# Two feed-forward units prepared twelve products sooner, and another order of copies, loads and transposes in the first row tiles

## The chip, the cores and the metric

One NeuronCore of a Trainium2 chip runs the kernel. A core has a matrix engine (TensorE, "PE"), three engines for elementwise work (VectorE "DVE", ScalarE "ACT", GpSimd "POOL"), a sync engine ("SP") that here only issues transfers, and 16 DMA engines. Every engine works off its own list of instructions in order; a transfer is issued by an engine and then runs by itself. The metric is the device time of one execution in microseconds, the median of several. Less is better.

## The reference

Two-branch encoder block, one layer, 1024 tokens of 1024 features, all in float32:

```python
h = rmsnorm(x, norm_mix)
q, k, v, r, lr_f, lr_b, u, g_a, g_b = split(h @ w_in)
o = gla(q, k, v, decay(lr_f)) + gla_backward(q, k, v, decay(lr_b))   # 4 heads, chunks of 64
y_a = (rmsnorm_per_head(o) * gla_norm * silu(r)) @ w_branch_gla
y_b = (pool_2_4_8_16(u) @ w_pool_group) * pool_scale                 # 4 channel groups
x = x + (sigmoid(g_a) * y_a + sigmoid(g_b) * y_b) @ w_out
gate, up = split(rmsnorm(x, norm_ffn) @ w_ffn_in)                    # 2816 wide each
x = x + (silu(gate) * up) @ w_ffn_out
return rmsnorm(x, norm_final)
```

## The kernel before

**Arithmetic.** A float32 operand is kept as two reduced-precision parts: `hi`, its cast (made on ACT), and `lo`, the difference between it and `hi` (made on DVE or POOL). One product of two operands is then three matmuls, hi·hi, lo·hi (or hi·lo) and the other cross product; `products` (L291) issues these three, and `mm3` calls it and then `pump`. Larger products use the Strassen–Winograd scheme of seven smaller products, for which sums and differences of the operands' quarters are made first.

**Order of the work.** The program is written out by a Python script whose main thread is the list of matmuls. Everything else hangs on generators that `pump(dt)` moves forward each time a triple of matmuls is issued: `dt` is the width over 512, so a triple of 512 columns is worth 1, and one of 288 columns 0.56. `begin(gen, delay)` puts a generator in the list `side`: it starts after `delay` of such credit, and each number it yields is the credit until its next step. `prepare_beside(jobs, every, put, lag, eng)` puts one in the list `aside`, a step per `every` of credit. `finish_side()` and `finish_beside()` issue at once all that is left of either list. So a number such as `every` sets where in each engine's list an instruction stands; how long it takes or waits there is another matter.

**First row tiles (0 to 47 us).** x arrives in eight tiles of 128 rows, `load_x(t)`. `norm_x(t)` scales a tile by its norm. `to_features` (L352) transposes two neighbouring tiles on PE, in four steps of four transposes (L338), and after each step `gain_and_split` makes the `hh` parts (ACT, L345) and `hl` parts (DVE, L348) of two feature tiles. `first_values` (L414) multiplies one row tile by the 288 columns of `w_in` that hold 256 values of the first head and 32 low-rank decay columns (`VL`, eight triples of 288 columns), and then takes the sum out of its PSUM bank: `vh` (ACT), `vl` (DVE, L199), and `lr`, four copies of the low-rank rows (ACT, L421). The low-rank columns of the weights come as one tile, `lraw` (L384, 128 KB in runs of 128 bytes), apart from the values' columns (`raw`), and POOL splits them (L249) into the `fwh` and `fwl` tiles that ACT and POOL also fill with the values' part. While `first_values` of t=1 runs, `to_features` of tiles 2 and 3 runs beside it, and so on by pairs.

**Gate units (381 to 582 us).** Ten units of seven products each; a product is 12 triples of 512 columns. Units 0 and 1 (kind "u") make the pooling branch's input, 2 to 5 the gate of branch A, 6 to 9 that of branch B. `Gates.run(p)` takes a product's bank: `ga` is filled by a copy on ACT (L1277), by an addition on DVE (L1282), by a sigmoid on ACT (L1285). Units of kind "b" also multiply the pooled rows `ph`, `pl` (loaded back from `p_out` by `load_pooled`, L1219) by the group's weights `wph`, `wpl` into a bank `yb`. The unit's weights come by SP in blocks named `fraw` too (L914 waits for one and makes the sum `fs`); their `wh` parts are casts on ACT (L198).

**Feed-forward units prepared ahead.** `unit_jobs(n)` (L559) is the job list of one feed-forward unit: load two raw tiles `fraw` (512 KB each, on SP), two blank steps, then seven jobs that make the operands of the unit's seven products. `beside` (L607) turns each job into steps: an optional sum or difference on POOL, `lag` steps later a cast `uph` (ACT, L627), a step later the difference `upl` (DVE, L618), and a step later (`put` = 1) the two stores to the DRAM tile `u_out` (L614) on the queue of the engine `eng`, here ACT's. `uph` and `upl` share a ring of five buffers (tag t2) with the rows of the pooling. Two units (`READY` = 2) are prepared this way; the feed-forward stage reads them back some 200 us later. At the start of unit 7 of the gates this list is begun; before the last unit `finish_beside()` empties it.

The lines of the gate loop that set this:

```python
for n, run in enumerate(gate_runs):
    last = n == len(gate_units) - 1
    if n == 7:
        finish_side()
        finish_beside()
        prepare_beside(map(unit_jobs, range(READY)), 3.1, 1, 2, nc.scalar)
    if last:
        finish_beside()
    for at, (of, p) in enumerate(run):
        zs[of].run(p)
```

After the gates come branch A's projection and the merge (582 to 770 us), the feed-forward units (770 to about 1180 us) and the output projection with the final norm (to 1393 us).

Of the kernel before, what the change touches and what calls it, by code (L numbers as in the profile page):

```python
# [52 lines left out]
def kernel(  # L53
# [57 lines left out]
    def as_f32(ap):  # L111
        return ap.bitcast(F32)
# [74 lines left out]
    def begin(gen, delay=0.0):  # L187
        side.append([gen, delay])
# [8 lines left out]
    def split_to(hi, lo, src, eng=nc.vector):  # L197
        nc.scalar.copy(hi, src)  # L198
        eng.tensor_tensor(lo, src, as_f32(hi), op=ALU.subtract)  # L199
# [149 lines left out]
                lo[:, c], src, g, as_f32(hi[:, c]), op0=ALU.mult, op1=ALU.subtract  # L349
            )  # L350

    def to_features(xn, t0, act, gain):  # L352

        for kp in range(KT // 2):
            ps = bank(ps_g, "tr")
            for i in range(2):
                transpose_tile(ps, xn[i], i, kp)
            gain_and_split(ps, kp, t0, act, gain)
            yield 1


    xt = [slot(shape=(D,), s="x") for _ in range(4)]
# [7 lines left out]
    def load_x(t):  # L370
        nc.sync.dma_start(xt[t % 4][:, :], x[t * P : (t + 1) * P, :])

    def load_rows(tile, at, v, n):
        nc.sync.dma_start(tile[at : at + n, :], v[0].rearrange("(j p) -> j p", p=P))
# [4 lines left out]

    load_x(0)  # L380
    load_rows(rows[0], 0, norm_mix, 8)
    load_x(1)
    first_raw = load(*next(order))
    nc.sync.dma_start(lraw[:, :, :], w_in[:, LR0:U0].rearrange("(k p) c -> p k c", p=P))  # L384
    for t in (2, 3):
        load_x(t)
    for i, (v, n) in enumerate(vec_rows):
# [27 lines left out]
    def first_values(w, v, t):  # L415

        ps = bank(ps_mm)
        for kt in range(KT):
            mm3(ps[:, :VL], tokens(hT(kt, t // 4), t), w(kt), kt == 0, kt == KT - 1)
        split_to(*(part[:, t % 4, :] for part in v[t // 4]), ps[:, :DV])  # L420
        nc.scalar.copy(low_rows[:, t, :, :], ps[:, DV:VL].unsqueeze(1).broadcast_to([P, 4, 2 * RANK]))  # L421

    def transpose_low(t):

# [44 lines left out]
    for t in range(0, NT, 2):  # L469
        if t + 4 < NT:  # L470
            begin(norms(t + 4), 1)
        if t == 2:
            for d, w_up in enumerate((w_decay_up_fwd, w_decay_up_bwd)):
                for i in range(3):
                    load_up(i, d, w_up)
            fetch()
        first_values(w, v, t)
        finish_side()
        if t == 0:
            vectors(1, 8)  # L480
        if t + 2 < NT:
            begin(to_features(xn[(t + 2) % 4 :], t + 2, hT, g_mix), 0.5)
        first_values(w, v, t + 1)
        finish_side()
        if t == 4:
            up_weights()
            prepare()
# [38 lines left out]
        return w[k0 : k0 + 2 * P, c_half * HALF : (c_half + 1) * HALF].rearrange("(k p) c -> p k c", p=P)  # L526


    def loading(srcs, tiles):
        def loads():  # L530
            for t, src in zip(tiles, srcs):
                nc.sync.dma_start(t, src)

        yield loads, None, None
        for _ in range(2):
            yield None, None, None


# [21 lines left out]
    def unit_jobs(n):  # L560
        raw = [slot(F32, (KT, P), "fraw")[:, :, :] for _ in range(2)]
        a11, a12, a21, a22 = (t[:, 4 * j : 4 * j + 4, :].rearrange("p k c -> p (k c)") for t in raw for j in range(2))
        yield from loading(
            [w_ffn_in[:, c0 : c0 + P].rearrange("(k p) c -> p k c", p=P) for c0 in (f_order[n] * P, D_FF + f_order[n] * P)], raw
        )
        for op, p, src in (
            (None, 4, a22), (None, 1, a11), (None, 2, a12), (partial(padd, a22, a21, a22), 5, a22),
            (partial(psub, a21, a11, a21), 7, a21), (partial(psub, a11, a22, a11), 6, a11),
            (partial(psub, a12, a12, a11), 3, a12),
        ):  # L570
            yield op, src, u_out[n][p]
# [33 lines left out]
    def beside(jobs, every, put, lag, eng):  # L605

        casts, differ = [None] * lag, None  # L607
        puts = [[] for _ in range(put)]
        while True:
            job = next(jobs, None)  # L610
            if not any((job, *casts, differ, *puts)):
                return
            for pair in puts.pop(0):
                eng.dma_start(*pair)  # L614
            puts.append([])
            if differ:
                src, (hi, lo), dst = differ
                nc.vector.tensor_tensor(lo, src, as_f32(hi), op=ALU.subtract)  # L618
                if len(src.shape) == 2:
                    puts[-1] += [(dst[:, i, :], as_f32(t)) for i, t in enumerate((hi, lo))]  # L620
                else:
                    right.setdefault(dst, []).append((hi, lo))
            differ, cast = None, casts.pop(0)
            if cast:
                src, dst = cast
                parts = parts_for(src)
                nc.scalar.copy(parts[0], src)  # L627
                differ = src, parts, dst
            casts.append(None)
            if job:  # L630
                op, src, dst = job
                if op:
                    op()  # L633
                if src is not None:
                    casts[-1] = src, dst
                elif dst is not None:

                    puts[-1].append((dst, op.args[0]))
            yield every
# [677 lines left out]
    for n, run in enumerate(gate_runs):  # L1317
        zs[n] = Gates(n)
        last = n == len(gate_units) - 1
        if n == 0:  # L1320
            prepare_beside(map(output_jobs, range(4)), 2.8, eng=nc.scalar)
        if n == 7:
            finish_side()
            finish_beside()
            prepare_beside(map(unit_jobs, range(READY)), 3.1, 1, 2, nc.scalar)
        if last:
            finish_beside()
        for at, (of, p) in enumerate(run):
            if not gates_ahead.step() and at in (5, 7):
                line_make()  # L1330
            zs[of].run(p)
            if at in (1, 2) and not last:
                gunits[n + 1].load()
            if p in (7, 4):
                zs[of].store(int(p == 4))
            if at == 4:
                flush(nc.scalar)
                if n == 2:
                    begin(pooling(), 4)
            if 5 <= n < 9 and at == 5:  # L1340
                load_pool_weights(n - 5)
            elif n >= 6 and at == 2:
                split_pool_weights(n - 6)
            if n >= 6 and at == (0 if last else 3):
                load_pooled(n - 6)
            if last and at == 1:
                load_block(0, 0)
                line_load()
                line_load()
                load_block(1, 0)  # L1350
            elif last and at == 2:
                line_load()
                line_load()
                load_block(0, 1)
                load_block(1, 1)
# [534 lines left out]
```

## Time and profile before

| what | value |
|---|---|
| time, median of 3 runs | 1395.01 us (1394.94 to 1395.22) |
| time of the profiled execution | 1394.28 us |
| its span (first to last instruction) | 1392.6 us |
| PE busy | 1366.0 us (98%) in 6654 instructions |
| ACT busy | 624.4 us (45%) |
| DVE busy | 844.0 us (61%) |
| POOL busy | 750.8 us (54%) |
| mean granted TensorE clock | 0.997 of full |

The profiled execution thus spent 1.68 us outside its span, and lies 0.73 us under the median. PE is busy nearly throughout, so whatever the change brings or costs must show as idle time of PE, as matmuls at a lower clock, or as a change in the number of matmuls. The profile gives each of them by place: the waits by engine and what ended them, the windows by stretch of time with their granted clock, the timeline by instruction.

### The profile page before, as it was taken

Reading aid. Unit: us, or ns where it says so; the run is one execution under the profiler, and the core shown is the slowest. Engines: PE = TensorE matmul, PEld = TensorE weight load, DVE = VectorE, ACT = ScalarE, POOL = GpSimd, SP = SyncE. Lnnn points to the kernel's source line nnn. Section 1 sums busy time; section 2 is a strip of 40 time slices with the busy share of each in tenths; the row PEclk is TensorE's granted clock in tenths of the full one; section 3 lists DMA queues with packets and bytes.
Section 4 is the critical chain, followed back from the end, with each engine's and each line's share of the span. In section 5 each row is a group of like instructions: output and inputs, shape, how many; then the busy total and the mean of one; then the engine's idle time right before and its main releaser. Section 6 shows DMA issues by size and latency. Waiting matters only on the chain.

```text
span 1392.6 us, 18505 instructions
## 1 busy us (share of the span) xinstructions
PE 1366.0 (98%) x6654; PEld 1153.0 (83%) x6654; DVE 844.0 (61%) x1073; ACT 624.4 (45%) x1125; POOL 750.8 (54%) x565
## 2 busy tenths in 40 slices
PE   7999999999999999999999999999999999999997
PEld 6889899988888888788887888888888888888876
DVE  6276767767635875587874866555655556343363
ACT  6364655644334444454346533333333334453253
POOL 3260716312397545568664276666766667454354
PEclk9999999999999999999999999999999999999999
DMA  6221422321486668997415455555444447975461
GB/s 192 76 81 37 126 72 96 121 77 46 137 274 233 207 204 275 332 404 261 151 61 212 140 178 174 174 174 168 154 138 143 149 141 265 386 257 210 166 237 66
DMA packets 167452, 243.56 MB, mean 175 GB/s; under 512 B 10904, under 2 KB 97856, under 8 KB 167360
## 3 DMA queue, kind: packets, MB, share of 16 engines
q1 hardware_dynamic: 154944, 216.16, 46.5%
q10 hardware_dynamic: 12416, 26.22, 5.1%
q8 instruction: 52, 0.85, 0.2%
q14 instruction: 40, 0.33, 0.1%
HBM read 164.48 MB, written 77.86 MB: 174 GB/s over the span
## 4 chain that ended last, share of the span: by engine, by line
PE 80%; DVE 5%; issue 5%; POOL 4%; DMA 3%; ACT 2%; SPq 0%; ACTq 0%; POOLq 0%; DVEq 0%
PE ps L291 74%; POOL wl L199 2%; PE op L845 2%; PE kv L291 1%; PE sc L773 1%; DMA wor<-t_out 1%; DMA u_out<-uph 1%; PE op L291 1%; PE tp L1004 1%; DVE fs L914 0%; DMA raw<-in_w_in_dram 0%; DMA ph<-p_out 0%; DVE x L1568 0%; PE yb L291 0%; POOL wsum L633 0%
## 5 line engine op out<-in xcount | busy, mean ns | idle before, releaser
L199 POOL TENSOR_TENSOR wl<-fs,wh 128x512 fp32r<-128x512 f32 x120 | 164.9, 1379 | 164.1 <-ACT wh L198 136.2
L291 PE MATMUL ps<-gh,wh 128*128 128x512 f32 x616 | 240.7, 391 | 0.0
L291 PE MATMUL ps<-gl,wh 128*128 128x512 f32 x616 | 240.1, 390 | 0.4 <-DVE gl L1484 0.4
L291 PE MATMUL ps<-gh,wl 128*128 128x512 f32 x616 | 240.1, 390 | 0.0
L199 POOL TENSOR_TENSOR wl<-fraw,wh 128x512 fp32r<-128x512 f32 x90 | 129.9, 1444 | 66.1 <-ACT wh L198 65.3
L199 POOL TENSOR_TENSOR ol<-gor,oh 128x1024 fp32r<-128x1024 f32 (+1 forms) x42 | 100.3, 2394 | 93.0 <-ACT oh L198 70.4
L291 PE MATMUL ps<-hh,wh 128*128 128x512 f32 x376 | 150.1, 399 | 0.0
L199 POOL TENSOR_TENSOR wl<-raw,wh 128x512 fp32r<-128x512 f32 x44 | 64.0, 1470 | 158.1 <-ACT wh L198 158.1
L291 PE MATMUL ps<-hh,wl 128*128 128x512 f32 x376 | 146.8, 390 | 0.0
L291 PE MATMUL ps<-hl,wh 128*128 128x512 f32 x376 | 146.7, 390 | 0.0
L291 PEld LDWEIGHTS ps<-gl,wh 128*128 128x128 f32 x616 | 115.7, 188 | 24.5 <-DVE gl L1484 0.8
L291 PEld LDWEIGHTS ps<-gh,wl 128*128 128x128 f32 x616 | 115.7, 188 | 24.3 <-DMA wl<-u_out 0.4
L291 PEld LDWEIGHTS ps<-gh,wh 128*128 128x128 f32 x616 | 115.7, 188 | 23.8 <-DMA wh<-u_out 0.3
L291 PE MATMUL ps<-oh,oh 128*128 128x512 f32 x308 | 120.1, 390 | 1.2 <-DVE x L1812 1.2
L291 PE MATMUL ps<-ol,oh 128*128 128x512 f32 x308 | 120.1, 390 | 0.2 <-DVE ol L199 0.2
L291 PE MATMUL ps<-oh,ol 128*128 128x512 f32 x308 | 120.0, 390 | 0.0
L199 POOL TENSOR_TENSOR wl<-wraw,wh 128x512 fp32r<-128x512 f32 x56 | 90.2, 1638 | 47.5 <-ACT wh L198 47.3
L199 DVE TENSOR_TENSOR ol<-wor,oh 128x1024 fp32r<-128x1024 f32 (+1 forms) x42 | 62.2, 1501 | 53.7 <-ACT oh L198 46.4
L198 ACT CAST wh<-fs 128x512 fp32r<-128x512 f32 x120 | 73.8, 615 | 30.8 <-DVE fs L914 23.1
L291 PEld LDWEIGHTS ps<-hh,wl 128*128 128x128 f32 x376 | 70.6, 188 | 14.9
L291 PEld LDWEIGHTS ps<-hh,wh 128*128 128x128 f32 x376 | 70.9, 189 | 13.3
L291 PEld LDWEIGHTS ps<-hl,wh 128*128 128x128 f32 x376 | 70.9, 189 | 13.2
(258 smaller groups left out, 3171.0 us busy)
## 6 DMA issues: line engine op xcount, KB each, us to landing
fraw<-in_w_ffn_in_dram SPq DMA_DIRECT2D x44, 512.0 KB, 6.4
gor<-g_out SPq DMA_DIRECT2D x35, 512.0 KB, 7.4
raw<-in_w_in_dram SPq DMA_DIRECT2D x48, 256.0 KB, 3.5
g_out<-s SPq DMA_DIRECT2D x44, 256.0 KB, 2.3
fraw<-in_w_in_dram SPq DMA_DIRECT2D x20, 512.0 KB, 5.1
wor<-t_out SPq DMA_DIRECT2D x20, 512.0 KB, 7.9
g_out<-g SPq DMA_DIRECT2D x33, 256.0 KB, 2.5
x<-in_x_dram SPq DMA_DIRECT2D x16, 512.0 KB, 4.4
```

The lines of the kernel that those rows point to most:

```text
L198: nc.scalar.copy(hi, src)
L199: eng.tensor_tensor(lo, src, as_f32(hi), op=ALU.subtract)
L291: nc.tensor.matmul(ps, a[i], b[j], start=first and n == 0, stop=last and n == 2, skip_group_check=onto)
L773: nc.tensor.matmul(sc[d][:, i * CH : (i + 1) * CH], chunk_of(ke, n, d), chunk_of(qe, n, d), start=True, stop=True,)
L845: nc.tensor.matmul(op[:, :DV], a, b, start=False, stop=j == len(terms) - 1)
L1004: nc.tensor.transpose(tp[:, i * P : (i + 1) * P], o_heads[j // 2][half][:, i, (j % 2) * P : (j % 2 + 1) * P], ident[:, :],)
```

## The change

Four things are moved; no operation is added or left out.

1. The two feed-forward units are begun twelve triples of matmuls sooner: after the fifth product of gate unit 6 in place of the start of unit 7. A step comes every 2.7 credits, not 3.1; the cast follows the sum by one step, not two; after a unit's load there are four blank steps, not two. The `hi` store is issued right behind its cast, and the `lo` store alone is left to a step later.
2. `lraw` is loaded ahead of x's second tile and of the first weights.
3. In `first_values`, `lr` is copied right after `vh`; `vl` is written out behind it.
4. In `to_features` of tiles 2 and 3 the first step starts after 2.2 credits, not 0.5, and the next ones follow by 0.6, not 1.

```diff
@@ -349,14 +349,14 @@
                 lo[:, c], src, g, as_f32(hi[:, c]), op0=ALU.mult, op1=ALU.subtract
             )
 
-    def to_features(xn, t0, act, gain):
+    def to_features(xn, t0, act, gain, every):
 
         for kp in range(KT // 2):
             ps = bank(ps_g, "tr")
             for i in range(2):
                 transpose_tile(ps, xn[i], i, kp)
             gain_and_split(ps, kp, t0, act, gain)
-            yield 1
+            yield every
 
 
     xt = [slot(shape=(D,), s="x") for _ in range(4)]
@@ -379,9 +379,9 @@
 
     load_x(0)
     load_rows(rows[0], 0, norm_mix, 8)
+    nc.sync.dma_start(lraw[:, :, :], w_in[:, LR0:U0].rearrange("(k p) c -> p k c", p=P))
     load_x(1)
     first_raw = load(*next(order))
-    nc.sync.dma_start(lraw[:, :, :], w_in[:, LR0:U0].rearrange("(k p) c -> p k c", p=P))
     for t in (2, 3):
         load_x(t)
     for i, (v, n) in enumerate(vec_rows):
@@ -417,8 +417,10 @@
         ps = bank(ps_mm)
         for kt in range(KT):
             mm3(ps[:, :VL], tokens(hT(kt, t // 4), t), w(kt), kt == 0, kt == KT - 1)
-        split_to(*(part[:, t % 4, :] for part in v[t // 4]), ps[:, :DV])
+        hi, lo = (part[:, t % 4, :] for part in v[t // 4])
+        nc.scalar.copy(hi, ps[:, :DV])
         nc.scalar.copy(low_rows[:, t, :, :], ps[:, DV:VL].unsqueeze(1).broadcast_to([P, 4, 2 * RANK]))
+        nc.vector.tensor_tensor(lo, ps[:, :DV], as_f32(hi), op=ALU.subtract)
 
     def transpose_low(t):
 
@@ -479,7 +481,7 @@
         if t == 0:
             vectors(1, 8)
         if t + 2 < NT:
-            begin(to_features(xn[(t + 2) % 4 :], t + 2, hT, g_mix), 0.5)
+            begin(to_features(xn[(t + 2) % 4 :], t + 2, hT, g_mix, 1 if t else 0.6), 0.5 if t else 2.2)
         first_values(w, v, t + 1)
         finish_side()
         if t == 4:
@@ -526,13 +528,13 @@
         return w[k0 : k0 + 2 * P, c_half * HALF : (c_half + 1) * HALF].rearrange("(k p) c -> p k c", p=P)
 
 
-    def loading(srcs, tiles):
+    def loading(srcs, tiles, blank=2):
         def loads():
             for t, src in zip(tiles, srcs):
                 nc.sync.dma_start(t, src)
 
         yield loads, None, None
-        for _ in range(2):
+        for _ in range(blank):
             yield None, None, None
 
 
@@ -561,7 +563,7 @@
         raw = [slot(F32, (KT, P), "fraw")[:, :, :] for _ in range(2)]
         a11, a12, a21, a22 = (t[:, 4 * j : 4 * j + 4, :].rearrange("p k c -> p (k c)") for t in raw for j in range(2))
         yield from loading(
-            [w_ffn_in[:, c0 : c0 + P].rearrange("(k p) c -> p k c", p=P) for c0 in (f_order[n] * P, D_FF + f_order[n] * P)], raw
+            [w_ffn_in[:, c0 : c0 + P].rearrange("(k p) c -> p k c", p=P) for c0 in (f_order[n] * P, D_FF + f_order[n] * P)], raw, 4
         )
         for op, p, src in (
             (None, 4, a22), (None, 1, a11), (None, 2, a12), (partial(padd, a22, a21, a22), 5, a22),
@@ -617,7 +619,7 @@
                 src, (hi, lo), dst = differ
                 nc.vector.tensor_tensor(lo, src, as_f32(hi), op=ALU.subtract)
                 if len(src.shape) == 2:
-                    puts[-1] += [(dst[:, i, :], as_f32(t)) for i, t in enumerate((hi, lo))]
+                    puts[-1].append((dst[:, 1, :], as_f32(lo)))
                 else:
                     right.setdefault(dst, []).append((hi, lo))
             differ, cast = None, casts.pop(0)
@@ -625,6 +627,8 @@
                 src, dst = cast
                 parts = parts_for(src)
                 nc.scalar.copy(parts[0], src)
+                if len(src.shape) == 2:
+                    eng.dma_start(dst[:, 0, :], as_f32(parts[0]))
                 differ = src, parts, dst
             casts.append(None)
             if job:
@@ -1319,10 +1323,6 @@
         last = n == len(gate_units) - 1
         if n == 0:
             prepare_beside(map(output_jobs, range(4)), 2.8, eng=nc.scalar)
-        if n == 7:
-            finish_side()
-            finish_beside()
-            prepare_beside(map(unit_jobs, range(READY)), 3.1, 1, 2, nc.scalar)
         if last:
             finish_beside()
         for at, (of, p) in enumerate(run):
@@ -1337,6 +1337,10 @@
                 flush(nc.scalar)
                 if n == 2:
                     begin(pooling(), 4)
+                if n == 6:
+                    finish_side()
+                    finish_beside()
+                    prepare_beside(map(unit_jobs, range(READY)), 2.7, 1, 1, nc.scalar)
             if 5 <= n < 9 and at == 5:
                 load_pool_weights(n - 5)
             elif n >= 6 and at == 2:
```

**ACT's list at the end of the gates.** Before, from the last sigmoid ahead of the last unit to the copy of that unit's first product. `uph`, `upl` are the feed-forward units' parts, `u_out_*_668` and so on the tiles they are stored to, `ga` the gate rows, `wh` a weight part of the last unit, and rows with DMA are transfers that ACT issues:

```order
L1285 ACTIVATE ga_5564<-ga_5564 128x512
L614 DMA u_out_2_668<-uph_5673 128x512
L614 DMA u_out_2_668<-upl_5674 128x512
L627 CAST uph_5720<-fraw_5524 128x512
L614 DMA u_out_5_671<-uph_5697 128x512
L614 DMA u_out_5_671<-upl_5698 128x512
L627 CAST uph_5731<-fraw_5523 128x512
L614 DMA u_out_7_673<-uph_5720 128x512
L614 DMA u_out_7_673<-upl_5721 128x512
L627 CAST uph_5737<-fraw_5523 128x512
L614 DMA u_out_6_672<-uph_5731 128x512
...
L198 CAST wh_5745<-fraw_5566 128x512
L1277 COPY ga_5767<-ps_5751 128x512
```

The row of "..." holds three more stores. The same place of the changed kernel (its L1281 is the copy that was L1277, L629 the cast, L631 the `hi` store, L616 the `lo` store):

```order
L629 CAST uph_5688<-fraw_5481 128x512
L631 DMA u_out_6_672<-uph_5688 128x512
L616 DMA u_out_7_673<-upl_5666 128x512
L629 CAST uph_5704<-fraw_5481 128x512
L631 DMA u_out_3_669<-uph_5704 128x512
L1289 ACTIVATE ga_5550<-ga_5550 128x512
L198 CAST wh_5712<-fs_5681 128x512
L616 DMA u_out_6_672<-upl_5689 128x512
L1289 ACTIVATE ga_5569<-ga_5569 128x512
L616 DMA u_out_3_669<-upl_5705 128x512
L198 CAST wh_5745<-fraw_5571 128x512
L1281 COPY ga_5767<-ps_5751 128x512
```

Before, three casts and ten stores stand between the last sigmoid and the copy `ga_5767`. Now one store stands there; the rest has moved up among the products of the unit ahead.

**PE's list in the second row tile's values.** The difference of the two lists in `first_values` of t=1; `tr` are the transposes of tiles 2 and 3 (`xn_132`, `xn_133`), `ps_308` is the bank of t=1:

```order
-L338 MATMUL tr_327<-ident,xn_132 128x128 x2
-L338 MATMUL tr_327<-ident,xn_133 128x128 x2
 L291 MATMUL ps_308<-fwh_206,hh_234 128x288
 L291 MATMUL ps_308<-fwl_207,hh_234 128x288
 L291 MATMUL ps_308<-fwh_206,hl_235 128x288
+L338 MATMUL tr_321<-ident,xn_132 128x128 x2
+L338 MATMUL tr_321<-ident,xn_133 128x128 x2
 L291 MATMUL ps_308<-fwh_208,hh_240 128x288
 L291 MATMUL ps_308<-fwl_209,hh_240 128x288
 L291 MATMUL ps_308<-fwh_208,hl_241 128x288
```

Before, the transposes of tiles 2 and 3 stand behind the first, third, fifth and seventh triple of the tile; now behind the fourth, fifth, seventh and eighth.

**SP's list at the start.** `x_126` to `x_129` are x's tiles, `raw_*` the values' columns of the first weights:

```order
 L371 DMA x_126<-in_x_dram 128x1024
 L374 DMA rows<-in_norm_mix_dram 8x128
+L382 DMA lraw_137<-in_w_in_dram 128x8x32
 L371 DMA x_127<-in_x_dram 128x1024
-L206 DMA raw_141<-in_w_in_dram 128x2x256
-L206 DMA raw_143<-in_w_in_dram 128x2x256
-L206 DMA raw_145<-in_w_in_dram 128x2x256
-L206 DMA raw_147<-in_w_in_dram 128x2x256
-L384 DMA lraw_137<-in_w_in_dram 128x8x32
```

One transfer, `lraw`, is moved past x's second tile and four transfers of weights.

## The prediction

> **What bounds the kernel now.** I read the busy line of the page first, then the waits of PE, then windows and the timeline round each longer wait.
>
> ```profile
> PE 1366.0 (98%) x6654; PEld 1153.0 (83%) x6654; DVE 844.0 (61%) x1073; ACT 624.4 (45%) x1125; POOL 750.8 (54%) x565
> PE ps L291 <- ACT ga L1277: 2.9, 1, 2.9
> PE yb L291 <- DMA pl<-p_out: 0.5, 1, 0.5
> PE ps L291 <- DVE ga L1282: 0.5, 1, 0.5
> ```
>
> PE is busy for 1366.0 of 1392.6 us, so only 26.6 us of idle time, and what the clock costs, can be won anywhere. The columns of the waits are total, times, longest. The longest single wait behind the start is one of 2.9 us for the copy `ga` (L1277); 0.5 us goes to the load of `pl`, and 0.5, in the whole run, to the additions of `ga` on DVE. Windows (stretch, length, then PE, weight loads, DVE, ACT, POOL, the granted clock, DMA share, GB/s) and timeline round the long one:
>
> ```profile
> 562.44:568.57 6.13, 6.13 (x28) 4.89 (x26) 3.50 (x5) 2.26 (x5) 3.18 (x2) 1.00 0.69 252
> 571.60:576.51 4.91, 4.91 (x14) 3.87 (x15) 3.24 (x5) 3.22 (x7) 4.91 (x4) 0.65 1.01 395
> 562.44 0.39 PE L291 MATMUL ps<-trh,wh 128*128 128x512 f32 x1
> 568.35 0.40 PE L291 MATMUL yb<-ph,wpl 128*128 128x512 f32 x1
> 571.60 0.50 PE L291 MATMUL ps<-trh,wh 128*128 128x512 f32 x1 [2.86 <-ACT ga L1277]
> 572.94 0.63 PE L291 MATMUL ps<-trh,wl 128*128 128x512 f32 x1
> 575.50 0.63 PE L291 MATMUL ps<-trh,wl 128*128 128x512 f32 x1
> 576.51 0.39 PE L291 MATMUL ps<-hh,wl 128*128 128x512 f32 x1
> ```
>
> Undisturbed, 27 matmuls start in 6.13 us (the 28th straddles the edge), 0.227 us each. From 568.35 to 576.51 there are 15 starts, the one at 568.35 and the window's 14; they cost 8.16 us in place of 15 x 0.227 = 3.4. So this one place loses **4.8 us**: 3.0 in the gap (571.60 − 568.35 − 0.227) and 1.7 behind it, where the granted clock is 0.65 and rows of 0.63 us stand 0.43 apart ((575.50 − 572.94) / 6).
>
> What made the copy late is on ACT:
>
> ```profile
> 568.27 0.62 ACT L627 CAST uph<-fraw 128x512 fp32r<-128x512 f32 x1 [1.26 <-DMA u_out<-upl]
> 569.84 0.56 ACTq L614 DMA_DIRECT2D u_out<-upl  x1
> 570.45 0.62 ACT L198 CAST wh<-fraw 128x512 fp32r<-128x512 f32 x1 [1.56 <-DVE fs L914]
> 570.97 0.58 ACT L1277 COPY ga<-ps 128x512 f32<-128x512 f32 x1
> DVE upl L618 <- DMA u_out<-uph: 9.8, 6, 3.0
> ACT uph L627 <- DMA u_out<-upl: 6.7, 5, 1.8
> DVE fs L914 <- DMA fraw<-in_w_in_dram: 2.7, 1, 2.7
> SPq L1219 <- DMA u_out<-uph: 16.4, 1, 16.4
> ```
>
> The copy's bank is full by 562.44, when PE goes on to the next product, yet ACT reaches it at 570.97, 8.5 us later; PE needs the bank after 27 more matmuls, 6.1 us. ACT stood in the emptied list of casts and stores: a cast waits until an earlier store has landed, a store until DVE's difference is made, DVE's until another store has landed (9.8 us in six waits between 525 and 575 us, ACT's 6.7 in five). The last row is SP's queue: the load of `ph`, `pl` waited 16.4 us for a store that has nothing to do with it, so issues here wait for transfers of other queues too, and that delays the loads of the next unit (`fs`, 2.7).
>
> **The gate units.** The change takes no cast, difference or store away; it moves them. Fourteen casts at 0.62 us and 28 stores stand in both kernels. The second row is for the `hi` stores, the third for the `lo` stores:
>
> ```profile
> L627 ACT CAST uph<-fraw x14: 614/621/629, 528.0 to 568.3; 128x512 fp32r<-128x512 f32 x14
> DMA to landing us min/median/max: 2.2/2.7/2.9
> DMA to landing us min/median/max: 2.9/3.9/4.9
> 510.00:530.00 20.00, 20.00 (x90) 16.48 (x89) 8.30 (x12) 8.50 (x16) 9.33 (x8) 1.00 0.81 249
> ```
>
> They begin 36 matmuls sooner, 36 x 0.227 = 8.2 us, so the first cast comes near 520, in a stretch in which ACT is busy for 8.50 of 20 us and POOL for 9.33. A step shrinks from 3.1 to 2.7 triples, 2.1 to 1.8 us; with the four added blank steps and the shorter lag it is some 27 steps in place of 24, so 49 us of list as against 50. Before, the last unit cut it short; now it begins 8.2 us sooner and fits. Placed by steps, the last `lo` store stands ahead of the last unit, with one `wh` cast and one copy behind it, so ACT should reach the copy within 2 us of its bank being full: 4 us of slack under PE's 6.1. Stalls inside the list get short: a cast then waits for a `hi` store issued two steps (3.6 us) before, which lands in 2.7; a difference waits for a `lo` store of two steps before, landing in 3.9, up to 1.3 late at the worst landing of 4.9. Behind it on DVE stand `fs` and the additions of `ga`; before, DVE stood up to 3.0 there in one wait, and PE waited 0.5 for those additions in all, so 1.3 should cost nothing. I take the whole 4.8. The lower bound is nothing (the burst moves, below).
>
> The `pl` wait of 0.5 sits ahead of the same loads. SP's 16.4 us for a store ends when the stores are spread, so I take 0.5 with bounds 0 and 0.7. POOL's sums come as quickly as the casts and may delay its weight parts `wl`; these stand some four steps, 7 us, ahead of their matmuls in the lists, so I cost that at nothing; uncovered, PE would wait for `wl`. Gate sum: **4.8 + 0.5 = 5.3**.
>
> [...]
>
> **The first row tiles.** Three edits, one chain:
>
> ```profile
> ACT lr L421 <- DVE vl L199: 10.7, 8, 3.2
> L421 ACT COPY lr<-ps x8: 265/265/268, 21.1 to 47.5; 128x128 f32<-128x128 f32 x8
> 17.82 0.44 PE L338 MATMUL tr<-ident,xn 128*128 128x128 f32 x2 [0.86 <-DVE n1rs L322]
> 20.64 0.42 DVE L199 TENSOR_TENSOR vl<-ps,vh 128x256 fp32r<-128x256 f32 x1
> 22.13 3.23 DVE L348 SCALAR_TENSOR_TENSOR hl<-tr,cols,hh 128x256 fp32r<-128x256 f32 x8 [0.97 <-ACT hh L345]
> 30.03 0.42 DVE L199 TENSOR_TENSOR vl<-ps,vh 128x256 fp32r<-128x256 f32 x1
> 31.53 3.23 DVE L348 SCALAR_TENSOR_TENSOR hl<-tr,cols,hh 128x256 fp32r<-128x256 f32 x8 [1.07 <-ACT hh L345]
> 22.20:30.60 8.40, 8.36 (x66) 8.11 (x64) 5.55 (x14) 5.08 (x14) 1.10 (x2) 1.00 0.52 140
> 30.60:35.10 4.50, 3.79 (x27) 3.34 (x26) 3.56 (x9) 3.34 (x10) 0.00 (x0) 1.00 0.00 0
> ```
>
> `lr` first: eight times ACT stood behind `vl`, 10.7 us in all, and the `hh` copies behind it. Now `vl` waits for `lr`, 0.265 us each. Queued behind `vl` on DVE are `hl` and the norms' scaling, for which PE waits; but `vl` at 20.64 and 30.03 starts late because of DVE's own norms, long after `lr` could be done, so there the new wait costs nothing (bounds 0 and 0.27 each). At t=4, DVE's `hl` sat idle 1.07 us for `hh` before 31.53; with `hh` free earlier it starts right behind `vl`, near 30.45. The stretch of t=4 took 4.50 us for 27 matmuls, at the 0.127 of the stretch before (8.36 / 66) 3.43: **1.1** lost, all of it to a chain that now comes 1.1 sooner or more. At t=2 the same, 0.97 sooner.
>
> Later transposes: the wait of 0.86 at 17.82 is for tile 3's norm. The transposes now follow the fourth triple, three triples of 3 x 0.127 later, 1.1 us, so it would go. But what t=1 wins t=2 must be able to use: its `hl` start near 21.1 and follow in 0.40 us (3.23 / 8) against 0.38 for a triple. That is enough if the norms are on time.
>
> `lraw` first is where they may not be:
>
> ```profile
> 9.84 0.62 ACT L198 CAST fwh<-raw 128x512 fp32r<-128x512 f32 x1 [0.26 <-DMA raw<-in_w_in_dram]
> 10.61 0.77 POOL L249 CAST fwh<-lraw 128x64 fp32r<-128x64 f32 x4 [2.43 <-DMA lraw<-in_w_in_dram]
> lraw<-in_w_in_dram SPq DMA_DIRECT2D x1, 128.0 KB, 6.4
> DMA packets 2947, 3.90 MB, mean 279 GB/s; under 512 B 1223, under 2 KB 2287, under 8 KB 2947
> ```
>
> Before, POOL's part starts at 10.61, when `lraw` has landed, ACT's last part at 9.84. Turned round, the weights and x's second tile land later by what `lraw` takes: 128 KB at 279 GB/s is 0.47 us, at most the 0.77 between those two starts. ACT's `hh`, its squares and DVE's norms all move by it, while POOL is ready earlier. I take 0.5 for it, so the first part comes out even and tile 3's wait shrinks by 0.86 − 0.5, some **0.4**. Start sum: 1.1 + 0.4 = **1.5**; at the best 0.9 + 1.1 + 0.4 for POOL's earlier parts = 2.4, at the worst −0.8 (0.77 late, nothing won).
>
> [...]
>
> **Sum.** 5.3 + 1.5 = 6.8. The profiled execution took 1394.28, so 1387.5 on its basis; the median of the runs lies 0.7 above it: **1388.2**.
>
> **Rivals.**
>
> *The start wins nothing or loses up to 0.8* (lraw's transfer delays norms and weights as much as the rest gains): 1395.0 − 5.3 = 1389.7, up to 1390.5. For it: at the start everything waits on transfers. Against: the gap at t=4 is a chain of ACT and DVE, long after.
>
> *Part of the gap stays.* In the changed program one `lo` store, that of the first unit's sixth job, waits on the counter on which the second unit's raw load counts. One such load takes
>
> ```profile
> fraw<-in_w_ffn_in_dram SPq DMA_DIRECT2D x44, 512.0 KB, 6.4
> ```
>
> so ACT may stand up to some 4 us there, as SP did for its 16.4. PE's slack is 6.1, but with other lateness 1 to 3.5 of the 4.8 may stay, or the clock's 1.7 alone, and 0.9 of the start with it: 1389.2 to 1392.6.
>
> *The change doesn't do what it says*: the same stores, sooner, still put ACT 8.5 us behind, at another product. Then 1395.0, less up to 1.5: 1393.5 to 1395.2. For it: steps come faster (1.8 us) than `lo` lands (3.9).
>
> *Slower.* The mechanism is that same held store, in both units. Once ACT comes more than 6.1 us late to a copy, PE stops, and each stop costs what this one did, 4.8 with its clock. One store held a full landing of 6.4 behind its issue, on top of a `wh` cast, passes that point. Two stops in place of one, 9.6, with the start's 1.5 and the 0.5 kept: 1388.2 + 9.6 = 1397.8. Against it: only one store among 28 stands so, and its load has been under way for some time when ACT comes to it.
>
> **How the numbers follow.** Forecast 0.60, start empty 0.13, part of the gap 0.13, no effect 0.08, slower 0.06. The forecast's own range goes from 1395.0 − 5.5 − 2.4 = 1387.1, less the 0.5 of DVE's additions, to 1389.7. The range takes in the first three cases, 0.86: 1386.6 to 1392.6. About 0.2%, 2.8 us, is what a measurement of this kernel can tell from no change; below 1392.2 lie the forecast, the empty start and two thirds of the third case, 0.82; within 2.8 us the rest of that and the fourth, 0.12; above, the last, 0.06.
>
> **What would show it.** PE's wait for `ga` (2.9) gone from its list, no stretch with a clock under 0.95 between 520 and 590, SP's long wait for `u_out` gone: the gate step holds. `lr` no longer waiting for `vl`, no wait of PE for `hh` or `hl` near 30 us: the copies' step holds. ACT's last `fwh` later than 9.84 and POOL's first earlier than 10.61 measure `lraw`. Wrong I would be if ACT waits in its own queue for a raw load between 530 and 550, or if PE waits for `wl` or `ga` anywhere in 520 to 582.

## The result, and the profile after

| kernel | median, us | runs | lowest to highest |
|---|---|---|---|
| before | 1395.22 | 6 | 1394.94 to 1396.55 |
| changed | 1389.88 | 6 | 1388.75 to 1390.84 |

The ratio is 0.9961, with a 95% interval of 0.995 to 0.9971: 5.3 us faster, 0.4%. The profiled execution of the changed kernel took 1389.96 us with a span of 1388.2, 4.3 us less than that of before (1394.28). The accounts below are made between these two traces.

The page's busy line, and the waits of PE (total, times, longest; the line numbers have moved, L1281 is the copy of `ga` that was L1277):

```profile
PE 1363.7 (98%) x6654; PEld 1152.1 (83%) x6654; DVE 849.1 (61%) x1073; ACT 624.7 (45%) x1125; POOL 754.4 (54%) x565
PE tr L338 <- DVE xn L327: 2.9, 2, 2.3
PE ps L291 <- ACT ga L1281: 1.5, 1, 1.5
```

The wait for `ga` has not gone from the list, it has shrunk from 2.9 to 1.5. The waits for `pl`, `hh` and `hl` are gone. The 2.9 in two times for `xn` is 2.3 as before and a new 0.6. The timeline of PE shows that the wait for `ga` is not the old one:

```profile
553.06 0.39 PE L291 MATMUL ps<-hh,wl 128*128 128x512 f32 x1
554.96 0.50 PE L291 MATMUL ps<-trh,wh 128*128 128x512 f32 x1 [1.51 <-ACT ga L1281]
...
568.55 0.40 PE L291 MATMUL yb<-ph,wpl 128*128 128x512 f32 x1
568.79 0.39 PE L291 MATMUL ps<-trh,wh 128*128 128x512 f32 x1
569.01 0.40 PE L291 MATMUL ps<-trl,wh 128*128 128x512 f32 x1
```

At 568.79 stands the matmul that stood idle until 571.60 before: it now follows 0.24 us behind its neighbour, and the clock behind it stays full (granted 1.00 from 16.25 to 1385.00 us of this trace; before, 0.50 from 572.76 to 576.18). Some 14 us earlier, in the gate unit ahead, PE stops at a place where it did not stop before, 1.67 us over the usual step and 0.11 more at the restart.

Laid side by side, matmul for matmul, the two traces differ like this (minus: the changed kernel is ahead):

| place | before, us | after, us | difference |
|---|---|---|---|
| first product of t=1 | 16.09 | 17.41 | +1.32 |
| first product of t=7, the last row tile | 43.23 | 41.91 | −1.32 |
| behind a first, short stop | 542.53 | 541.56 | −0.97 |
| behind the new stop | 554.12 | 554.96 | +0.84 |
| the old gap's matmul | 571.60 | 568.79 | −2.82 |
| behind the old half clock | 575.93 | 571.52 | −4.41 |
| last matmul | 1385.28 | 1380.96 | −4.32 |

So t=0 is 1.3 us slower, t=1 to t=6 are 2.6 faster, 0.3 goes at 541, a new stop takes 1.8, and the old place gives back 5.2. After the gates small gains and losses, up to 0.6, even out.

**What holds the new stop.** ACT's timeline ahead of it:

```profile
545.62 0.62 ACT L629 CAST uph<-fraw 128x512 fp32r<-128x512 f32 x1 [0.41 <-ACT uph L629]
546.27 0.33 ACTq L631 DMA_DIRECT2D u_out<-uph  x1
...
547.96 0.62 ACT L629 CAST uph<-fraw 128x512 fp32r<-128x512 f32 x1
548.61 0.33 ACTq L631 DMA_DIRECT2D u_out<-uph  x1
549.81 0.33 ACTq L616 DMA_DIRECT2D u_out<-upl  x1
553.31 0.62 ACT L629 CAST uph<-fraw 128x512 fp32r<-128x512 f32 x1 [4.73 <-DVE fs L918]
553.95 0.33 ACTq L631 DMA_DIRECT2D u_out<-uph  x1
554.32 0.58 ACT L1281 COPY ga<-ps 128x512 f32<-128x512 f32 x1 [0.40 <-ACT uph L629]
```

The copy stands behind a cast that sat idle for 4.73 us. The row blames `fs` on DVE, but a cast reads no `fs`. In the program it waits for its input, the sum that POOL makes one step before, and for the `hi` store of two jobs before, whose buffer has to come free. POOL's sum was made at 551.01. The store was issued at 546.27; in the trace its counter rises by sixteen, one event at a time, the last of them at 553.23, 7.0 us after the issue, and the cast starts 0.08 behind that. So the store held the cast for the last 2.2 us.

The short stop at 541 has a like cause, on DVE:

```profile
540.02 0.88 DVE L620 TENSOR_TENSOR upl<-fraw,uph 128x512 fp32r<-128x512 f32 x1 [3.87 <-DMA u_out<-upl]
540.83 0.68 DVE L1286 TENSOR_TENSOR ga<-ps,ga 128x512 f32<-128x512 f32 x1
```

The difference waited 3.87 us for a `lo` store that was issued at 533.03 and landed at 539.90, 6.9 us later; the addition behind it ends at 541.51, and PE, which waits for that bank, goes on at 541.56.

The windows show how full the DMA was meanwhile, the third row in the trace of before (stretch, length, PE, weight loads, DVE, ACT, POOL, granted clock, DMA share, GB/s):

```profile
545.00:549.00 4.00, 4.00 (x20) 3.28 (x19) 2.17 (x3) 2.76 (x6) 3.34 (x3) 1.00 0.81 203
549.00:555.00 6.00, 4.49 (x21) 3.41 (x19) 2.69 (x3) 1.30 (x3) 3.62 (x3) 1.00 1.05 407
549.00:555.00 6.00, 6.00 (x28) 4.98 (x27) 2.15 (x4) 3.46 (x7) 2.54 (x2) 1.00 1.07 382
```

From 549 to 555 the DMA engines are full (share 1.05) and move 407 GB/s, but before they were as full (1.07, 382 GB/s). The tiles' views of the changed kernel give what stores took from issue to landing, `uph` and then `upl`:

```profile
DMA to landing us min/median/max: 2.2/3.5/4.8
```

```profile
DMA to landing us min/median/max: 3.5/4.9/8.7
```

These rows stand on the few stores that the view could pair with their events: 2 of the 14 `hi` stores and 3 of the 14 `lo` stores here, 3 and 2 of them before. Read by the last of the sixteen events of its counter, every one of the 28 stores can be told. Before, `hi` stores took 2.0 to 9.4 us with a median of 2.9, `lo` stores 2.0 to 9.5 with a median of 3.5; in the changed kernel it is 2.0 to 7.7 with 5.0, and 3.5 to 8.7 with 6.1. Before, the two stores that were issued ahead of the full stretch, at 546.97 and 548.85, took 5.8 and 6.8 us.

### The profile page after: what moved, and what is told of

The parts are those of the page before. It is cut to its first block, busy times and chain, and to the rows that moved or that the text cites. A ratio compares the mean times of both kernels' runs of the same rounds, so it can differ in the third digit from the quotient of the medians.

```text
span 1388.2 us, 18504 instructions
## 1 busy us (share of the span) xinstructions
PE 1363.7 (98%) x6654; PEld 1152.1 (83%) x6654; DVE 849.1 (61%) x1073; ACT 624.7 (45%) x1125; POOL 754.4 (54%) x565
## 5 line engine op out<-in xcount | busy, mean ns | idle before, releaser
L291 PEld LDWEIGHTS ps<-hh,wh 128*128 128x128 f32 x376 | 70.7, 188 | 13.2
L291 PEld LDWEIGHTS ps<-hl,wh 128*128 128x128 f32 x376 | 70.7, 188 | 13.2
```

Source lines behind the costliest of these rows:

```text
L291: nc.tensor.matmul(ps, a[i], b[j], start=first and n == 0, stop=last and n == 2, skip_group_check=onto)
```

## The experiments

Twelve kernels ran, each timed beside the kernel before on its chip; the medians of before there were 1395.16 (the first four), 1395.80 (the next four) and 1395.68 (the last four).

| run | median, us | ratio to before, 95% interval |
|---|---|---|
| gate units' part alone | 1391.60 | 0.9977 (0.9968 to 0.9986) |
| first row tiles' part alone | 1393.57 | 0.9988 (0.9980 to 0.9997) |
| lraw back | 1388.18 | 0.9954 (0.9940 to 0.9967) |
| a step every 3.1 | 1391.23 | 0.9972 (0.9963 to 0.9981) |
| six buffers | 1387.10 | 0.9940 (0.9928 to 0.9953) |
| one product sooner, steps of 2.9 | 1387.78 | 0.9942 (0.9929 to 0.9954) |
| hi store beside lo | 1393.56 | 0.9985 (0.9976 to 0.9994) |
| lr behind vl | 1392.55 | 0.9978 (0.9967 to 0.9989) |
| feature steps undone | 1390.54 | 0.9965 (0.9955 to 0.9975) |
| sooner, lraw back | 1387.49 | 0.9942 (0.9928 to 0.9957) |
| sooner, lraw back, six buffers | 1387.41 | 0.9944 (0.9931 to 0.9957) |
| the changed kernel again | 1389.19 | 0.9956 (0.9943 to 0.9969) |

**The two parts by themselves.** The first leaves out the edits to `lraw`, `lr` and the feature steps, the second the edits to `unit_jobs`, `beside` and the gate loop.

> Only the feed-forward units' preparation is changed (sooner start, steps of 2.7, lag 1, four blank steps, hi store behind its cast); the first row tiles are as before. Theory A (the two places add): the changed kernel's trace lies 3.1 us ahead of before from the gates on, of which 5.0 won at the old gap and 1.9 lost at a new one; so 1395.2 - 3.1 = 1392.1, with the new stop of PE at the copy of ga near 555 us still there. Rival B (the new stop comes of the shifted start, which moves loads against each other): no stop, 1390.2.

> Only the first row tiles are changed (lraw first, lr ahead of vl, later and shorter feature steps); the units' preparation is as before. Theory A: 1.3 us won by 32 us and kept, 1395.2 - 1.3 = 1393.9, with the old gap of 2.9 us near 570. Rival B: what is won at the start is eaten by the next wait, 1395.2.

The gate part alone is 3.6 us under before, the first row tiles' part 1.6, together 5.2, as the whole change in the first session (5.3). Theory A holds in both. The new stop is in the gate part's trace, the old gap in the other's.

```profile
PE ps L291 <- ACT ga L1279: 1.3, 1, 1.3
```

is the gate part's wait of PE, which ends at 557.09 us, and

```profile
569.80 0.50 PE L291 MATMUL ps<-trh,wh 128*128 128x512 f32 x1 [3.42 <-ACT ga L1279]
```

the start part's, in its timeline.

**Longer steps.**

```diff
-prepare_beside(map(unit_jobs, range(READY)), 2.7, 1, 1, nc.scalar)
+prepare_beside(map(unit_jobs, range(READY)), 3.1, 1, 1, nc.scalar)
```

> The changed kernel with a step every 3.1 triples in place of 2.7. Theory A (the new stop near 555 comes of casts and differences that wait for stores landing late on a full DMA, so longer steps give the stores time): the stop of 1.5 us goes or shrinks under 0.5, and what is left of the list, some three steps at the last unit, costs under 1; 1389.0. Rival B (the list is again cut by the last unit, so the burst comes back): a gap of 1 to 3 near 568, 1391 to 1393.

Half of theory A: with slower steps the stop near 555 is gone, and PE's one wait between 500 and 590 us is the 2.42 below. What it said of the end was wrong: the rest of the list fell on the last unit, as rival B has it, and PE stood there again.

```profile
565.62 0.40 PE L291 MATMUL yb<-ph,wpl 128*128 128x512 f32 x1
568.44 0.50 PE L291 MATMUL ps<-trh,wh 128*128 128x512 f32 x1 [2.42 <-ACT ga L1281]
...
569.34 0.63 PE L291 MATMUL ps<-trh,wh 128*128 128x512 f32 x1
...
571.90 0.63 PE L291 MATMUL ps<-trh,wh 128*128 128x512 f32 x1
```

After 2.42 us idle the matmuls stand 0.43 apart again. With this start, steps of 3.1 are not done in time, and steps of 2.7 are, at the price of the new stop; no run tried a rate between the two.

**More buffers.**

```diff
-    tmp = ctx.enter_context(tc.tile_pool(name="tmp", bufs=5))
-    small = ctx.enter_context(tc.tile_pool(name="small", bufs=5))
+    tmp = ctx.enter_context(tc.tile_pool(name="tmp", bufs=6))
+    small = ctx.enter_context(tc.tile_pool(name="small", bufs=4))
```

> The changed kernel with six buffers in the ring that uph and upl share, not five (and, to make room, four in place of five in the small ring that holds the pooling weights' parts). All transfers stay. Theory A (PE's stop near 555 comes of a cast that waits until a hi store issued 7 us before has left its buffer, ahead of the copy of ga in ACT's list): the cast finds a buffer free, the stop of 1.5 us goes, 1.5 faster than the changed kernel, 1388.4, unless the small ring costs something in the attention. Rival B (POOL's sums or the raw loads set the cast's time): the stop stays at 1.3 or more.

PE has no wait between 500 and 590 us in this trace. The same place on ACT:

```profile
548.13 0.60 ACTq L616 DMA_DIRECT2D u_out<-upl  x1
550.57 0.62 ACT L629 CAST uph<-fraw 128x512 fp32r<-128x512 f32 x1 [2.89 <-POOL fraw L637]
551.22 0.33 ACTq L631 DMA_DIRECT2D u_out<-uph  x1
551.59 0.59 ACT L1281 COPY ga<-ps 128x512 f32<-128x512 f32 x1 [0.40 <-ACT uph L629]
```

The same cast, with the same stores and loads under way, now starts when POOL's sum is ready, 2.7 us earlier, and the copy with it; 0.9 of the 2.7 is that ACT's list is ahead already (the cast before stands at 547.06 against 547.96). The `hi` store of two jobs before, issued at 545.38, landed only at 551.72, 6.3 us later and 1.1 behind the start of this cast, which no longer needs its buffer. The buffer was the cause; theory A holds. The time is 2.8 under the changed kernel's first median and 2.1 under its second, both taken in other sessions; the stop and the 0.3 at 541, which is gone too, make 2.1. The small ring cost nothing that can be seen.

**Sooner and slower.**

```diff
-                if n == 6:
+            if n == 6 and at == 3:
...
-                    prepare_beside(map(unit_jobs, range(READY)), 2.7, 1, 1, nc.scalar)
+                prepare_beside(map(unit_jobs, range(READY)), 2.9, 1, 1, nc.scalar)
```

> The changed kernel with the units begun one product of gate unit 6 sooner and a step every 2.9 triples. Theory A (stores that land late on a full DMA): less traffic in each stretch, the list ends 4 us sooner than in the changed kernel's plan, the stop near 555 falls under 0.7 and no burst is left for the last unit: 1389 or below. Rival B (the moment matters, not the rate: the raw loads of a unit now fall on the pooling's last transfers): a stop of 1 to 3 at another place, 1390 to 1392.

No wait of PE between 500 and 590 here either, so rival B falls. Casts still wait for stores, but elsewhere:

```profile
548.84 0.62 ACT L629 CAST uph<-fraw 128x512 fp32r<-128x512 f32 x1 [2.45 <-POOL fraw L637]
549.49 0.33 ACTq L631 DMA_DIRECT2D u_out<-uph  x1
549.86 0.59 ACT L1281 COPY ga<-ps 128x512 f32<-128x512 f32 x1 [0.40 <-ACT uph L629]
...
554.40 0.62 ACT L629 CAST uph<-fraw 128x512 fp32r<-128x512 f32 x1 [3.43 <-DMA u_out<-uph]
```

The order of casts and copy is that of the changed kernel; the late store has fallen to another cast. The one that the cast at 548.84 needs was issued at 544.08 and landed at 548.70, 4.6 us later and just ahead of POOL's sum. The next one took 7.9 us (546.42 to 554.32), and the cast that it holds stands behind the copy that PE needs. So in these two traces a stall of ACT is free or dear by what stands next in its list. "Less traffic" was not what helped: ACT's waits for `hi` stores were 8.2 us in four, against the 4.73 and one of 0.9 in the changed kernel. Nor does the list end 4 us sooner, as I had reckoned: one product is twelve matmuls, 2.7 us, and 27 steps, each longer by 0.2 triples, take 3.7 us more.

**The early hi store undone.** The edit puts both stores of a job on `puts` again.

```diff
-                    puts[-1].append((dst[:, 1, :], as_f32(lo)))
+                    puts[-1] += [(dst[:, i, :], as_f32(t)) for i, t in enumerate((hi, lo))]
...
-                if len(src.shape) == 2:
-                    eng.dma_start(dst[:, 0, :], as_f32(parts[0]))
```

> The changed kernel with the hi store issued beside the lo store again, a step after the difference. Theory A (casts wait for the landing of hi stores): hi stores come two steps, 3.6 us, later, so each cast waits longer, and the stop of PE grows from 1.5 to 3 or more: 1391.5 to 1394. Rival B (what counts is the traffic alone): same as the changed kernel, 1390.

Theory A, with two stops in place of one:

```profile
543.63 0.50 PE L291 MATMUL ps<-trh,wh 128*128 128x512 f32 x1 [1.97 <-DVE ga L1284]
...
558.50 0.50 PE L291 MATMUL ps<-trh,wh 128*128 128x512 f32 x1 [2.98 <-ACT ga L1279]
```

ACT's casts waited 16.3 us in this trace for `lo` stores, issued just behind the `hi` stores; the longest wait, 6.2 us, stands ahead of the second stop. The edit that looks smallest in the diff, the early `hi` store, is worth some 3 to 4 us: without it the rest of the change wins 2.2 against its session's before, with it 5.3 and 6.5 in two sessions.

**The first row tiles, piece by piece.** `lraw` back behind the first weights; `lr` behind `vl` again; the transposes of tiles 2 and 3 with a delay of 0.5 and a step of 1. Three kernels, an edit each:

```diff
-    nc.sync.dma_start(lraw[:, :, :], w_in[:, LR0:U0].rearrange("(k p) c -> p k c", p=P))
     load_x(1)
     first_raw = load(*next(order))
+    nc.sync.dma_start(lraw[:, :, :], w_in[:, LR0:U0].rearrange("(k p) c -> p k c", p=P))
```

```diff
-        hi, lo = (part[:, t % 4, :] for part in v[t // 4])
-        nc.scalar.copy(hi, ps[:, :DV])
+        split_to(*(part[:, t % 4, :] for part in v[t // 4]), ps[:, :DV])
         nc.scalar.copy(low_rows[:, t, :, :], ps[:, DV:VL].unsqueeze(1).broadcast_to([P, 4, 2 * RANK]))
-        nc.vector.tensor_tensor(lo, ps[:, :DV], as_f32(hi), op=ALU.subtract)
```

```diff
-            begin(to_features(xn[(t + 2) % 4 :], t + 2, hT, g_mix, 1 if t else 0.6), 0.5 if t else 2.2)
+            begin(to_features(xn[(t + 2) % 4 :], t + 2, hT, g_mix, 1), 0.5)
```

> The changed kernel with lraw's load back behind the first weights. Theory A (lraw's transfer delays x's second tile, which opens a gap of 0.9 us in the transposes and keeps the clock at half until 16 us in place of 13): the gap goes, the clock rises near 13 us, t=0 ends 1.4 us sooner; DVE's norms then set t=1, so 0.5 to 1.2 faster than the changed kernel, about 1389. Rival B (POOL's late part of the weights, 0.8 us of waits before, comes back and takes it): same as the changed kernel, 1389.9.

> The changed kernel with lr copied behind vl's difference again. Theory A (lr's wait held ACT's hh and squares): ACT waits 10 us for vl again, the gap of 1.0 at t=4 comes back near 31 us, and the wait at t=2 too: 1.0 to 2.0 slower than the changed kernel, 1391. Rival B (the later transposes did it): same as the changed kernel, 1390.

> The changed kernel with the transposes of tiles 2 and 3 after the first, third, fifth and seventh triple again. Theory A (the later transposes give tile 3's norm time): PE's wait of 0.9 to 1.0 for tile 3's norm at t=1 comes back, less what t=2 waited for hl, so 0.3 to 0.9 slower than the changed kernel. Rival B (with lr ahead of vl and a t=0 that ends 1.3 us later, the norm is on time anyway): same as the changed kernel.

`lr` behind `vl`: ACT waits again, and PE at t=4.

```profile
ACT lr L421 <- DVE vl L199: 10.5, 8, 3.0
```

```profile
PE ps L291 <- ACT hh L345: 0.4, 1, 0.4
PE ps L291 <- DVE hl L348: 0.6, 2, 0.4
```

From the first product of t=1 to that of t=7 it takes 26.32 us against 24.50 in the changed kernel: 1.8 for this order of two copies. Feature steps undone: 25.47 against 24.50, nearly all in t=1, where PE waits for tile 3's norm again:

```profile
18.19 0.44 PE L338 MATMUL tr<-ident,xn 128*128 128x128 f32 x2 [0.72 <-DVE n1rs L322]
```

So theory A holds in both, by the trace. The median of the second is 1.35 above the changed kernel's on the same chip (1389.19), but their runs overlap. `lraw` is less clear. In the trace with it back, x's second tile is squared at 6.11 us and the clock is full at 12.4, in the changed kernel's trace at 16.3; t=7 begins at 40.55, 1.4 sooner than in the changed kernel's trace. But with `lraw` back in the next two kernels the square came once at 7.46 and once at 6.32.

**What the pieces make together.** The sooner start with steps of 2.9 and `lraw`'s load back (the two edits above in one kernel), the same with six buffers, and the changed kernel itself.

> Both repairs that left every buffer as it was: units begun one product sooner with steps of 2.9, and lraw's load behind the first weights. Theory A (they add): no stop of PE for ga in the gates, x's second tile squared near 6.1 us; 1395.5 less 5.3 (gates) and 2.0 (start), 1386 to 1387.5. Rival B: the start's part does not add, 1387.8 as with the sooner units alone.

> The same with six buffers for uph and upl (and four in the small ring). Theory A (with the sooner start no cast that PE waits for is held by a buffer): same as with two repairs, within 0.5. Rival B (buffers still hold ACT, and with it DVE's additions of ga): 0.5 to 1 faster.

> The changed kernel itself, beside the three others on the same chip. All theories: 1389 to 1391, with the stop of 1.3 to 1.7 for ga near 555 and x's second tile squared after 7 us; the clock full either near 12.5 or near 16 us, which is worth about 1 us at the end of the first row tiles.

Both kernels lie some 1.7 under the changed kernel of their session and 0.3 and 0.4 under the sooner units alone: moving `lraw` back adds nothing that the medians can show, and theory A and rival B lie too close here to be told apart. Six buffers add nothing to the sooner start, theory A. The five runs with six buffers alone (1386.49 to 1388.69) have the lowest median; the four kernels without the stop cannot be told apart. All four beat both given kernels: their slowest runs, 1388.09 to 1388.76, are about the changed kernel's fastest, 1388.75. In the changed kernel's second trace the stop was 1.1 us, shorter than the 1.3 to 1.7 expected, and x's second tile was squared at 7.61.

## Why the prediction was right, and where not

The forecast was 1388.2, the time 1389.88: the sign is right, and the time lies inside the range of 1386.6 to 1392.6. It lies just above the forecast's own stretch, 1387.1 to 1389.7; the range holds it because two rivals were counted in. By traces the sum of 6.8 came out as 4.3 (1394.28 − 1389.96), by medians as 5.3.

**The old gap, 4.8: right.** The gap and the half clock behind it are both gone; from that matmul's neighbour to the end of the old half clock the changed kernel makes up the whole. `pl`, 0.5: right; PE has no such wait any more. SP's 16.4 us for a store of `u_out` is gone too, though SP's load of `ph` stood 13.7 us for a store of gate rows, `yb_out`.

**The step that failed** is the sentence on stalls inside the list: a `hi` store "issued two steps (3.6 us) before, which lands in 2.7", and a `lo` store "up to 1.3 late at the worst landing of 4.9". I took the landing times from rows that stand on 3 and 2 of 14 stores. The trace of before already had 5.8 and 6.8 us ahead of the full stretch at 549 to 555, the two stores issued at 546.97 and 548.85. In the changed trace the `hi` store took 7.0, the cast behind it stood 4.73, and a difference stood 3.87 for a `lo` store of 6.9.

The slack was too large as well. The copy of `ga` began 6.5 us after its bank was full (547.85 to 554.32). PE came back to that bank at 553.29, after 24 matmuls or 5.4 us, and the copy itself takes 0.58, so the slack was 4.9 and not the 6.1 of the old gap's 27 matmuls: 6.5 − 4.9 = 1.6 is the stop. With six buffers the copy began 3.7 us after (547.90 to 551.59), and PE did not wait. The cost, 1.8 and the 0.3 at 541, is what the gate sum lacked: 5.3 became some 3.1 (4.41 − 1.32). Six buffers take it away with all transfers left as they were. By its own sign, a wait of PE for `ga` in 520 to 582, this part of the prediction was wrong.

A smaller slip is the start of the list. A product of a gate unit is twelve matmuls, four triples, not twelve triples; from the fifth product of unit 6 to the start of unit 7 there are two products and three triples on the pooled rows, so the list begins 33 matmuls sooner, 7.5 us (507.67 to 515.21 in the trace of before), not 36 and 8.2.

The rival "part of the gap stays" gave 1389.2 to 1392.6 and is the case that came, but not by its mechanism. The `lo` store that waits on the raw load's counter did stand in the list: it was issued at 539.23, and that load (issued at 533.00) had landed at 539.21. It cost nothing that can be seen: ACT had ended its cast at 538.99, and the sigmoid behind, at 541.54, waited for DVE's addition at 540.83, which the other `lo` store had held. The dear store was the `hi` one with its buffer, which I had ruled out.

**Slower: not seen in the changed kernel, but the rival was near.** With the `hi` store put back, two stops of 1.97 and 2.98 us came, one per unit, as many as that rival had; its mechanism, a store held by a raw load, was not the one, since ACT's casts waited there for `lo` stores to land. Neither stop was followed by a lower clock (the mean granted clock of that run is 0.999, as in the changed kernel, against 0.997 before), and the kernel stayed 2.2 under before.

**The first row tiles: 1.5 against 1.3 measured, near by luck, since the terms were other ones.** The gap at t=4, 1.1: from the start of t=3 to that of t=5 the kernel went from 9.38 to 8.14 us, 1.2. Tile 3's wait, 0.4: t=1 went from 6.12 to 4.94, 1.2, and t=2 won 0.2 behind it; I had taken 0.5 off for `lraw`. "The first part comes out even": it lost 1.3. `lraw`'s 0.5 us of delay, bounded by 0.77, was 1.27 in this trace:

```profile
7.44 1.06 ACT L331 ACTIVATE xn<-x 128x1024 f32<-128x1024 f32 x1 [1.52 <-DMA x<-in_x_dram]
```

```profile
10.25 1.97 PE L338 MATMUL tr<-ident,xn 128*128 128x128 f32 x8 [0.62 <-DVE xn L327]
12.25 0.44 PE L291 MATMUL ps<-fwl,hh 128*128 128x288 f32 x1
```

x's second tile comes late, the transposes stand idle for 0.6 us at 9.6, and the matmuls behind are still 0.24 apart until 16.3; before, they were 0.13 apart from 13.0. Both the delay and the clock cost. In the trace of the start part alone the square came at 7.05, with the transposes 0.89 apart at the gap, and the clock was full at 12.2. There t=0 began at 11.43 and took 4.47 us; in the changed kernel it began at 11.87 and took 5.54, and before it began at 10.98 and took 5.11. So with the full clock from 12.2, the first part comes out even (t=1 at 15.90, before at 16.09); with the full clock from 16.3, some 1.1 us more go. Whether `lraw` in front causes the late tile stays open: with it in front the square came at 7.05 to 7.88 in all nine traces, behind the weights at 6.11, 6.17, 6.32, 7.46 and 7.53.

The delay of 1.27 is more than the 0.5 that I took for `lraw`, but the two late tiles without `lraw` in front (7.46 and 7.53) show that such a delay comes by itself too.

## What to carry to other kernels

Work that is put off the critical path still stands in some engine's list, and what it costs is set by what is queued behind it there: here a wait of ACT of 4.73 us ahead of a copy stopped PE for 1.51, and one of 3.43 behind that copy did not stop it. Before looking for less work, look for the buffer that the stalling instruction waits for: here one more buffer took the stop away, and so did a start by which the late store fell to a cast behind the copy that PE needs.

A landing time in a view can stand on two or three transfers of fourteen. Count them, or read the counters, before a buffer's return is put on the way to a copy, and take the longest landing of a full DMA stretch, not the median (here 7.7 us against 5.0 for `hi` stores, 8.7 against 6.1 for `lo`). The slack of a copy ends with the copy, not with its start (0.58 us later here). And where the profile names a releaser that the instruction doesn't read, look up what it waits for.

## What the runs showed of the hardware

**The clock behind a gap.** Idle stretches of PE of 2.42 us (longer steps), 2.86 (before) and 3.42 (start part alone) were each followed by seven steps of 0.43 us between matmuls in place of 0.23, which began 0.9 to 1.6 us behind the restart; in the trace of before the granted clock there is 0.50 for 3.41 us. One of 2.98 (hi store beside lo) and one of 1.51 (changed) were not: the mean granted clock of these two executions is 0.999, that of the other three 0.997. So in these five traces the length alone does not decide; what does was not shown.

**The clock at the start.** In the fourteen traces taken, the largest step between two transposes at the start and the time of the full clock, from which matmuls of 288 columns stand 0.13 us apart and not 0.24, go together (before 0.27 and 13.0, changed 1.05 and 16.3): steps of 0.27 to 0.92 us, full clock at 12.2 to 13.2; steps of 1.02 to 1.72, full clock at 14.0 to 16.6. With a tile that came a microsecond late the matmuls stayed 0.24 apart for 1 to 4 us longer; among the kernels with the same first row tiles, the two with the early full clock begin t=7 0.6 to 1.3 us sooner than the others (40.88 and 41.14 against 41.74 to 42.15). No run was made to change that gap alone, so this is a pattern, not a shown cause.

**Landing of stores.** A store of 256 KB to DRAM took 2.0 to 9.5 us from issue to its sixteenth event before, and 2.0 to 8.7 in the changed kernel; the longest ones were under way with the DMA engines full (before, 568.3 to 579.3 us: share 1.02, 347 GB/s; changed, 548.6 to 556.3 us: 1.04, 400 GB/s). That the load is the cause was not tried by a run of its own.
